# The first load of a row-maximum kernel in two halves of 64 partitions, issued from two queues

## The chip, the cores and the metric

The kernel runs on one core of one Trainium2 chip. The metric is the device time of one execution in microseconds (us). Three runs of the kernel before took 627.81 to 627.84 us, with a median of 627.82 us. The profile is of one further execution, which took 627.6 us.

## The reference

The input `x` is an 8192 x 8192 matrix of float32, 268.4 MB. The output has one number for each row: the largest absolute value in the row.

```python
def reference(x: np.ndarray) -> np.ndarray:
    return np.linalg.norm(x, ord=np.inf, axis=1)
```

So every byte of `x` has to be read once from device memory (HBM), and little is written: 32 KB.

## The kernel before

**Tiling.** On-chip memory (SBUF) has 128 partitions. The 8192 rows are taken in two groups (`GROUPS`): the first gives each partition 46 rows that follow each other in memory, the second 18. So each partition has 64 rows of 8192 numbers to work through, and what it reads for one load is one contiguous piece of memory. A "load" is a DMA of `w` numbers for every partition. The table `WHOLE` has 31 loads of 16384 numbers (two rows for each partition, 64 KB for each partition, 8.39 MB in all) and one of 8192. The table `LAST` cuts the last row of each partition into six shrinking loads of 3920 down to 320 and 352 numbers.

**Ring.** The data go to `ring`, a buffer of three slots of 64 KB for each partition, so three loads can be on their way or in use at once. The last piece of all goes to a small buffer, `last`. `load` (L97 on) finds the place in the ring, issues the DMA from SP's queue (L108), and keeps a list `loads` of the place and instruction of each load.

**Work.** For each whole load, VectorE (DVE) takes the largest absolute value of each row with one reduce (`absmax`, L68) over 128 x 16384 numbers. It writes two columns of `res`, which holds one result for each of the 64 rows of a partition. For the last two whole loads and for the pieces of the last row, `shared` splits the columns: DVE takes some, and ScalarE (ACT) makes the others absolute (L90) for GpSimd (POOL), which takes their maximum (L75). At the end one reduce joins the parts of the last row (`absmax` over `last`), SP writes its result column (L154) and ScalarE's queue writes the other 63 columns (L159).

**Order.** The engines' orders are those of the program (`keep`). SP does nothing but issue loads and the last store, in order. The first three loads wait for nothing. Each later load waits until the reduce that used its ring slot, three loads before, is over. A scheduler assigns the semaphores: DMAs take eight semaphores in turn, and an instruction that needs the data of a load waits for that load's semaphore. For some loads, chosen by `(len(loads) + 4) % 10 < 5`, the kernel declares that the new load need not wait for the earlier loads of the same slot themselves (the reduces in between order them); for the others SP has such a wait too, in an instruction of its own ahead of the load. ScalarE's first work is the load of its function table and one tiny activation (L140), which is made to wait for the second reduce, so that the table is there long before it is used at the end.

Of the kernel before, what the change touches and what calls it, by code (L numbers as in the profile page):

```python
# [1 line left out]

# [4 lines left out]

P = 128
FP32 = mybir.dt.float32
INT32 = mybir.dt.int32  # L10
MAX = mybir.AluOpType.max
X = mybir.AxisListType.X
ABS = mybir.ActivationFunctionType.Abs

GROUPS = [46, 18]


WHOLE = (
    [(16384, ())] * 30 + [(16384, (3712, 3680)), (8192, (2016, 1984))]
)
LAST = [
    (3920, (1680,)), (1984, (848,)), (1040, (432,)), (576, (240,)), (320, ()), (352, ())
]
RING = 3 * 16384


@with_exitstack  # L30
def kernel(
    ctx: ExitStack,
    tc: tile.TileContext,
    x: bass.AP,
    out: bass.AP,
):
    nc = tc.nc
    n_rows, n_cols = x.shape
    R = n_rows // P
    assert R == sum(GROUPS) and n_cols == 8192  # L40
    keep = tc.keep_in_program_order


    first = []
    x_of, out_of = {}, {}
    for k in GROUPS:
        f = len(first)
        x_of[f] = x[f * P : (f + k) * P].rearrange("(p r) m -> p (r m)", r=k)
        out_of[f] = out[f * P : (f + k) * P].rearrange("(p r) -> p r", r=k)
        first += [f] * k  # L50

    single = ctx.enter_context(tc.tile_pool(name="single", bufs=1))

    ring = single.tile([P, RING], FP32)
    res = single.tile([P, R], FP32)

    n_parts = sum(1 + len(g) for w, g in LAST[:-1])
    last = single.tile([P, LAST[-1][0] + n_parts], FP32)

    def not_before(inst, other, why):  # L60
        tc.add_manual_dep(
            inst.ins, other.ins.name,
            mybir.DependencyInfo(mybir.DependencyClass.Sync, mybir.DependencyReason.DATA),
            reason=why,
        )

    def absmax(dst, src):
        return keep(nc.vector.tensor_reduce(  # L68
            out=dst, in_=src, axis=X, op=MAX, apply_absolute_value=True,
        ))  # L70

    def max_pool(dst, src):

        pool = nc.gpsimd
        keep(pool.add_instruction(  # L75
            mybir.InstTensorReduce(
                name=nc.get_next_instruction_name(),
                ins=[pool.lower_ap(src.bitcast(INT32))],
                outs=[pool.lower_ap(dst.bitcast(INT32))],
                op=MAX,  # L80
                axis=X,
            )
        ))

    def shared(part, buf, g):

        a = buf.shape[1] - sum(g)
        red = absmax(part[:, :1], buf[:, :a])
        for i, c in enumerate(g):
            keep(nc.scalar.activation(buf[:, a : a + c], buf[:, a : a + c], ABS))  # L90
            max_pool(part[:, 1 + i : 2 + i], buf[:, a : a + c])
            a += c
        return red

    loads = []

    def load(pos, w):  # L97

        row = pos // n_cols
        a = pos - first[row] * n_cols  # L100
        if pos + w == R * n_cols:
            buf = last[:, :w]
        else:
            at = loads[-1][0] + loads[-1][1] if loads else 0
            if at + w > RING:
                at = 0
            buf = ring[:, at : at + w]
        inst = nc.sync.dma_start(out=buf, in_=x_of[first[row]][:, a : a + w]).ins  # L108
        if pos + w < R * n_cols:
            if (len(loads) + 4) % 10 < 5:  # L110


                for b, v, earlier in loads:
                    if b < at + w and at < b + v:
                        tc.declare_no_dep(
                            inst, earlier, reason="ordered by the reduces in between",
                        )
            loads.append((at, w, inst))
        return buf


    pos = 0
    for u, (w, g) in enumerate(WHOLE):
        buf = load(pos, w)
        row, k = pos // n_cols, w // n_cols
        pos += w
        whole = k - 1 if g else k
        if whole:
            red = absmax(
                res[:, row : row + whole],  # L130
                buf[:, : whole * n_cols].rearrange("p (c m) -> p c m", m=n_cols),
            )
        if g:
            part = single.tile([P, 1 + len(g)], FP32, name=f"part{u}")
            shared(part, buf[:, whole * n_cols :], g)
            max_pool(res[:, row + whole : row + k], part)
        if u == 1:

            not_before(
                keep(nc.scalar.activation(res[:, :1], res[:, :1], ABS)),  # L140
                red, "not before the second row is in",
            )


    n = LAST[-1][0]
    for h, (w, g) in enumerate(LAST[:-1]):
        buf = load(pos, w)
        pos += w
        shared(last[:, n : n + 1 + len(g)], buf, g)
        n += 1 + len(g)  # L150

    load(pos, LAST[-1][0])
    absmax(res[:, R - 1 :], last)
    final = nc.sync.dma_start(out=out_of[first[-1]][:, GROUPS[-1] - 1 :], in_=res[:, R - 1 :])  # L154


    for f, o in out_of.items():
        k = min(o.shape[1], R - 1 - f)
        early = keep(nc.scalar.dma_start(out=o[:, :k], in_=res[:, f : f + k]))  # L159
    tc.add_manual_dep(  # L160
        early.ins, final.ins.name,
        mybir.DependencyInfo(mybir.DependencyClass.NoSync, mybir.DependencyReason.SCHED_ONLY),
        reason="takes the later semaphore",
    )


# [1 line left out]
_INS = ['x']  # L168
_OUTS = [((8192,), 'float32')]


# [23 lines left out]
```

## Time and profile before

| what | value |
|---|---|
| median of three runs | 627.82 us |
| profiled execution, whole time | 627.6 us |
| profiled execution, span | 625.8 us |
| VectorE busy | 536.5 us, 86% of the span |
| ScalarE busy, GpSimd busy | 15.0 us, 14.1 us |
| moved by DMA | 268.47 MB, mean 429 GB/s |
| share of the 16 DMA engines' span that SP's queue took | 99.3% |
| one reduce of 128 x 16384 numbers | 17.22 us |
| issue of a load to its landing, median | 40.8 us |

The span is the time between the first and the last record of the core; the 1.8 us between it and the execution's time lie around it. "Busy" is the time in which an engine worked on an instruction; for DMA it is the time that packets took on the 16 DMA engines which all queues of the core share. A reader should keep in mind that a load's time to landing includes the time for which it stands behind earlier loads.

### The profile page before, as it was taken

What the parts mean: (1) busy time and instruction counts of PE and PEld (TensorE: products, weight loads), DVE (VectorE), ACT (ScalarE), POOL (GpSimd) and SP (SyncE); (2) the same over time, 40 slices, a digit from 0 to 9 for tenths busy, and PEclk for the clock granted to TensorE, in tenths of its full rate; (3) what the DMA queues carried; (4) which work ended last, traced back from release to release, by engine and by line L of the source; (5) the groups of instructions that cost most, each with busy time, mean ns of one, the idle gap of its engine ahead of it and who ended that gap; (6) DMA issues with size and microseconds to landing.
All of it is one profiled execution on the core that took longest, in us unless ns stands there. A gap on an engine that the chain in (4) does not pass through costs nothing.

```text
span 625.8 us, 173 instructions
## 1 busy us (share of the span) xinstructions
DVE 536.5 (86%) x39; ACT 15.0 (2%) x10; POOL 14.1 (2%) x14
## 2 busy tenths in 40 slices
DVE  0588988889888899888898888988889888899888
ACT  0000000000000000000000000000000000000044
POOL 0000000000000000000000000000000000000026
DMA  9999999999999999999999999999999999999997
GB/s 402 402 469 402 469 402 469 402 469 402 465 406 457 415 431 440 411 461 402 469 402 469 402 469 402 465 406 461 411 448 423 419 452 406 465 402 469 402 436 304
DMA packets 5904, 268.47 MB, mean 429 GB/s; under 512 B 1040, under 2 KB 1296, under 8 KB 1680
## 3 DMA queue, kind: packets, MB, share of 16 engines
q1 hardware_dynamic: 5616, 268.44, 99.3%
q10 hardware_dynamic: 288, 0.03, 0.0%
HBM read 268.44 MB, written 0.03 MB: 429 GB/s over the span
## 4 chain that ended last, share of the span: by engine, by line
DMA 71%; DVE 28%; SPq 0%; issue 0%; DVEq 0%
DMA ring<-in_x_dram 71%; DVE res L68 28%; DVE last L68 1%; SPq L108 0%; DVEq L68 0%
## 5 line engine op out<-in xcount | busy, mean ns | idle before, releaser
L68 DVE TENSOR_REDUCE res<-ring 128x2 f32<-128x16384 f32 (+1 forms) x31 | 525.3, 16944 | 86.7 <-DMA ring<-in_x_dram 86.7
L90 ACT ACTIVATE ring<-ring 128x3712 f32<-128x3712 f32 (+7 forms) x8 | 13.6, 1718 | 549.3 <-DMA ring<-in_x_dram 549.2
L75 POOL TENSOR_REDUCE part<-ring 128x1 int32<-128x3712 int32 (+3 forms) x4 | 10.1, 2562 | 607.8 <-ACT ring L90 607.8
L68 DVE TENSOR_REDUCE part<-ring 128x1 f32<-128x800 f32 (+1 forms) x2 | 5.5, 2748 | 0.1
L68 DVE TENSOR_REDUCE last<-ring 128x1 f32<-128x2240 f32 (+4 forms) x5 | 5.3, 1115 | 0.1
L75 POOL TENSOR_REDUCE last<-ring 128x1 int32<-128x1680 int32 (+3 forms) x4 | 3.4, 855 | 0.5 <-ACT ring L90 0.4
L140 ACT ACTIVATE res<-res 128x1 f32<-128x1 f32 x1 | 0.2, 202 | 57.3 <-DVE res L68 57.3
L140 ACT ACT_TABLE_LOAD x1 | 1.3, 1283 | 0.7 <-PEq L179 0.7
L68 DVE TENSOR_REDUCE res<-last 128x1 f32<-128x361 f32 x1 | 0.5, 529 | 0.1
L75 POOL TENSOR_REDUCE res<-part 128x1 int32<-128x3 int32 x2 | 0.4, 198 | 0.1
L179 POOL MEMSET const-float32-0.0<- 128x1 f32 x1 | 0.1, 100 | 0.2 <-issue 0.2
L179 POOL MEMSET const-bfloat16-1.0<- 128x1 bf16 x1 | 0.1, 103 | 0.0
L179 POOL MEMSET const-uint8-127<- 128x1 uint8 x1 | 0.1, 102 | 0.0
L179 POOL MEMSET const-float32-1.0<- 128x1 f32 x1 | 0.1, 99 | 0.0
## 6 DMA issues: line engine op xcount, KB each, us to landing
ring<-in_x_dram SPq DMA_DIRECT2D x1, 4096.0 KB, 31.2
ring<-in_x_dram SPq DMA_DIRECT2D x1, 1960.0 KB, 35.4
ring<-in_x_dram SPq DMA_DIRECT2D x1, 992.0 KB, 37.4
ring<-in_x_dram SPq DMA_DIRECT2D x1, 520.0 KB, 38.2
ring<-in_x_dram SPq DMA_DIRECT2D x31, 40.8
ring<-in_x_dram SPq DMA_DIRECT2D x1, 288.0 KB, 38.4
last<-in_x_dram SPq DMA_DIRECT2D x1, 176.0 KB, 38.3
ring<-in_x_dram SPq DMA_DIRECT2D x1, 160.0 KB, 38.3
```

Of the source, the lines that this page charges most:

```text
L68: return keep(nc.vector.tensor_reduce(out=dst, in_=src, axis=X, op=MAX, apply_absolute_value=True,))
L75: keep(pool.add_instruction(mybir.InstTensorReduce(name=nc.get_next_instruction_name(), ins=[pool.lower_ap(src.bitcast(INT32))], outs=[poo ...
L90: keep(nc.scalar.activation(buf[:, a : a + c], buf[:, a : a + c], ABS))
L140: keep(nc.scalar.activation(res[:, :1], res[:, :1], ABS)),
L179: nc = _bacc.Bacc("TRN2", target_bir_lowering=False, num_devices=1)
```

## The change

The first load alone is issued in two DMAs. The half for partitions 64 to 127 is issued by ScalarE's queue, ahead of ScalarE's table load, and the half for partitions 0 to 63 by SP, as SP's first DMA. Neither waits for anything. All other loads are as before, on SP's queue with 128 partitions. The list `loads` gets an entry for each half, so its length is greater by one for every later load, and so is the count of DMAs that take semaphores in turn: the choice `(len(loads) + 4) % 10 < 5` falls one load earlier, and each load's semaphore is the next one. The first reduce waits for two semaphores where it waited for one.

```diff
-        inst = nc.sync.dma_start(out=buf, in_=x_of[first[row]][:, a : a + w]).ins
+        src = x_of[first[row]][:, a : a + w]
+        n = P
+        if not loads:
+
+            n = P // 2
+            inst = nc.scalar.dma_start(out=buf[n:], in_=src[n:]).ins
+            loads.append((at, w, inst))
+        inst = nc.sync.dma_start(out=buf[:n], in_=src[:n]).ins
         if pos + w < R * n_cols:
             if (len(loads) + 4) % 10 < 5:
```

## The prediction

> **What bounds the kernel now.** I read the page's shares first, then the chain that ended last, then the waits, then the start. The page's parts 1 to 3:
>
> ```profile
> span 625.8 us, 173 instructions
> DVE 536.5 (86%) x39; ACT 15.0 (2%) x10; POOL 14.1 (2%) x14
> DMA  9999999999999999999999999999999999999997
> q1 hardware_dynamic: 5616, 268.44, 99.3%
> ```
>
> Transfers fill every slice; no compute engine does. The chain in order of time seems to say otherwise:
>
> ```profile
> 1.17 40.91 DMA ring<-in_x_dram
> 42.07 0.02 issue
> 42.10 17.23 DVE res L68
> 59.33 0.02 issue
> 59.34 40.77 DMA ring<-in_x_dram
> 100.11 0.02 issue
> 100.14 17.23 DVE res L68
> ...
> 582.18 35.44 DMA ring<-in_x_dram
> 617.63 0.02 issue
> 617.65 5.29 DVE last L68 x5
> ```
>
> It alternates, but one turn is 100.14 - 42.10 = 58.04 us for three loads, 19.35 us each: 8.39 MB / 19.35 us = 433.6 GB/s. A reduce takes 17.22 us. The chain passes through a reduce only because it releases the ring slot; the load issued then still stands behind 2.13 us of one load and all 19.35 us of the next, so 40.8 us to landing = 2.1 + 19.35 + 19.35. DVE is the one that waits:
>
> ```profile
> DVE res L68 <- DMA ring<-in_x_dram: 86.7, 31, 22.7
> SPq L108 <- DVE res L68: 526.2, 29, 19.0
> ```
>
> 86.7 us = 22.75 us for the first load and 30 waits of 2.13 us. So the bound is the DMA engines' own work: a microsecond more of it is a microsecond more in the end, and SP's waits for reduces are covered by about 21.5 us of queued work. The start:
>
> ```profile
> 0.73 1.28 ACT L140 ACT_TABLE_LOAD   x1 [0.73 <-PEq L179]
> 0.74 1.33 SPq L108 DMA_DIRECT2D ring<-in_x_dram  x3
> 22.75 17.22 DVE L68 TENSOR_REDUCE res<-ring 128x2 f32<-128x16384 f32 x1 [22.75 <-DMA ring<-in_x_dram]
> ```
>
> SP issues its three free loads within 1.33 us, and ScalarE comes to its first instruction at the same time, 0.73 us. In the trace's packet records each engine moves one partition's 64 KB at a time, eight per load, one after another: 19.35 / 8 = 2.42 us each. The first packets start at 1.83 to 2.34 us over the 16 engines, and an engine's second some 3.06 us after its first: a fill of about 0.64 us, paid once.
>
> [...]
> [...]
> [...]
> [...]
> [...]
>
> **The change part by part.**
>
> *Issue.* One SP issue of 64 rows for one of 128; one more on ScalarE. SP's take 0.33 to 0.43 us, ScalarE's two at the end 0.86 together, so 0.43. It stands ahead of the table load, which moves from 0.73 to about 1.16 us; behind that is only the activation at 59.35, which waits 57.34 us for a DVE reduce. Cost 0; uncovered it would be 0.43. The halves start side by side, so at most the later half's issue, under 0.5 us, could be lost or won at the start, out of 1.8 us before the first packet. I take 0.
>
> *The transfer of the first load.* The same 8.39 MB, eight packets per engine, now four from each queue. [...]a packet takes 2 x 2.42 = 4.84 us, eight take 38.7 us in place of 19.35. That is +19.3 us. [...]I take the middle, +18.2. The unknown is bounded below by 0 (full rate; a gain is excluded, since the rest of the kernel already shows the full rate) and above by 19.3 and another fill, about 20.
>
> [...]A load has landed when its slowest engine is done, and every later load again gives that engine its sixteenth, with no gap in which to catch up.
>
> *Where the delay goes.* The first reduce starts at about 41 us and ends at 58 in place of 40. Load 3, which waits for it, is late by 18.2 too. But loads 1 and 2, issued by 2.1 us, stand in SP's queue and are late by the same, so load 3 still finds 21.5 us ahead of it. No second loss, no recovery: the 2.13 us that DVE has to spare per load help nothing, since DMA is the bound.
>
> *Two semaphores for the first reduce.* One more wait instruction on DVE, whose like on SP takes 17 ns where it finds its semaphore ready: 0.02 us once, within the 2.13 us of DVE's waiting.
>
> *Shifted waits and semaphores.* In the built program SP's loads have the same kinds of waits, the undeclared ones one load earlier; each is for a DMA of eight, or three, loads before, whose data a past reduce has already used. The last store waits for the same load as before. ScalarE's first L90 and GpSimd's first L75 gain waits for the two halves, past for 560 us. SP's 14 extra wait instructions stand before loads which have 21.5 us of cover. Cost 0; uncovered, up to 14 x 1.74 us, the longest of them.
>
> *The tail* (from 617.65 on) has the same instructions, later by 18.2.
>
> Sum on the profiled execution: 627.6 + 0 + 18.2 + 0 = 645.8 us. The median of the runs lies 0.2 above it, so 646.0.
>
> **The rivals.**
>
> *A, the likeliest[...]*, 646.0, own range 643 to 648[...]. [...]Against: nothing in this trace shows sharing.
>
> *B, not slower[...].* [...]Then the load takes 19.35 us and the time is 627.8, give or take 0.5.[...]
>
> *C, a part: changing queues costs[...].* If there is no conflict, but an engine pays the fill of 0.64 us anew at each of seven changes: +4.5 us, 632.3.[...] Against the first: packets of one queue follow each other without a gap. Range 630.5 to 643.
>
> *D: ScalarE's half starts late* and takes turns with load 1 instead. Load 0 then lands later, but the bytes are the same; up to some 20 us of it changes only DVE's start, as SP's queue holds loads 1 and 2. [...]627.8; I put it with B.
>
> *E, faster:* only what lies before the first packet could go, 1.8 us, and splitting leaves most of it. By over 0.2% (1.25 us) hardly possible.
>
> **How the numbers follow.** A 0.68, C 0.12, B and D 0.18, E 0.02. A measurement of this kernel can tell about 0.2%, 1.25 us. A and C are slower by more than that: 0.80; same 0.18; faster 0.02. The time is A's, 646.0. A and C together are 0.80, so the range is theirs with a little above A's end, 630.5 to 648.5; B is left out.
>
> **What would show it.** Right: the first reduce starts near 41 us (between 38 and 43), the page's first two slices show about 230 GB/s instead of 402, a queue of ScalarE's has 4.19 MB more, packets of the first load take up to 4.8 us; then the waits of 2.13 us, the turn of 58.04 us and the five last reduces as before, only later. The DMA digits should stay 9[...]. B: the first reduce at 22.7 us, all else unmoved. C: between. Wrong in another way: a wait of 2.13 us that changed in the middle of the kernel, or a gap in the slices, which would mean that the shifted waits count; or a first reduce that is late while the end is not (D).

## The result, and the profile after

The changed kernel takes 647.76 us (median of five runs, 647.59 to 648.71) against 627.82 for the kernel before: a ratio of 1.0323, with a 95% interval from 1.0308 to 1.0337. It is slower by 19.9 us. The profiled execution took 647.65 us, with a span of 645.9 us, 20.1 us more than before.

The page's parts 1 to 3, with the moved GB/s of each fortieth of the span:

```profile
span 645.9 us, 177 instructions
DVE 536.5 (83%) x39; ACT 15.1 (2%) x10; POOL 14.2 (2%) x14
DMA  9979999999989999999999999999999999999997
GB/s 195 260 260 455 446 398 455 451 394 455 455 390 455 455 390 455 455 394 451 455 394 451 455 406 438 455 414 430 455 426 418 455 434 410 455 434 410 455 412 304
q1 hardware_dynamic: 5552, 264.24, 96.2%
q10 hardware_dynamic: 368, 4.23, 3.0%
```

The rate of the kernel before:

```profile
GB/s 402 402 469 402 469 402 469 402 469 402 465 406 457 415 431 440 411 461 402 469 402 469 402 469 402 465 406 461 411 448 423 419 452 406 465 402 469 402 436 304
```

The compute engines work as long as before (DVE 536.5 us in both). The DMA engines look as busy as before, too, and yet they move 195 and 260 GB/s in the first two slices, where it was 402 in each. The 7 in the third slice is no pause: the page counts a packet in the slice in which it starts, and in the packet records all 16 engines are busy throughout that slice. A busy digit tells that packets are under way, not how fast they move: in the stretches below, a share of 0.97 goes with 219 GB/s and with 415. ScalarE's queue, q10, now has 4.19 MB of the input.

The same two stretches of the kernel before and of the changed one show where all of it lies. The columns are the stretch, its length, the busy time of DVE, ACT and POOL with the number of instructions, the clock, the DMA share and the GB/s. First the kernel before:

```profile
0.00:43.00 43.00, 18.12 (x2) 1.28 (x1) 0.20 (x4) 1.00 0.97 415
43.00:600.00 557.00, 497.33 (x29) 0.20 (x1) 0.00 (x0) 1.00 1.00 434
```

And the changed kernel:

```profile
0.00:43.00 43.00, 0.17 (x1) 1.28 (x1) 0.20 (x4) 1.00 0.97 219
43.00:600.00 557.00, 497.53 (x29) 0.20 (x1) 0.00 (x0) 1.00 1.00 433
```

The first 43 us move 219 GB/s instead of 415 at the same DMA share; everything after runs at the old rate (433 and 434 GB/s). The timeline of the changed kernel at its start and the chain at its end:

```profile
0.73 1.65 SPq L115 DMA_DIRECT2D ring<-in_x_dram  x3
0.74 0.56 ACTq L113 DMA_DIRECT2D ring<-in_x_dram  x1
1.33 1.28 ACT L147 ACT_TABLE_LOAD   x1 [1.33 <-PEq L186]
42.83 17.22 DVE L68 TENSOR_REDUCE res<-ring 128x2 f32<-128x16384 f32 x1 [42.83 <-DMA ring<-in_x_dram]
61.97 17.22 DVE L68 TENSOR_REDUCE res<-ring 128x2 f32<-128x16384 f32 x1 [1.92 <-DMA ring<-in_x_dram]
```

```profile
602.08 35.45 DMA ring<-in_x_dram
637.53 0.02 issue
637.55 5.30 DVE last L68 x5
```

The first reduce starts at 42.83 us, 20.08 later than before. The second waits 1.92 us (before: 2.13), so 0.2 of that came back. The last pieces' reduces start 19.90 us later and take the same 5.3 us. The trace also has a record of every packet, which the page does not show. In these packet records, the packets of load 0 after each engine's first took:

```
                 packets took, min / median / max    first 16 packets start    load 0's last packet ends
kernel before            2.42 / 2.42 / 2.42 us           1.74 to 2.25                 22.4
changed kernel           4.84 / 4.85 / 5.00 us           2.07 to 3.06                 41.9
```

In the changed kernel each of the 16 engines takes a packet of SP's queue first, then one of ScalarE's, and so on, four of each. So all engines work on the same half, except for the 1.3 us over which their changes from one queue to the other are spread. Each packet takes twice the time of before (4.85 us for 2.42). Only the first packets do not: before, the first took 3.16 us on average, 0.7 more than the others, and now it takes 4.88, hardly more than the others. The extra time comes up in the first packets of load 1 instead, which take 3.05 us for 2.42.

### The profile page after: what moved, and what is told of

Same layout as the page of the kernel before. It is cut to its first block, busy times and chain, and to the rows that moved or that the text cites. A ratio compares the mean times of both kernels' runs of the same rounds, so it can differ in the third digit from the quotient of the medians.

```text
span 645.9 us, 177 instructions
## 1 busy us (share of the span) xinstructions
DVE 536.5 (83%) x39; ACT 15.1 (2%) x10; POOL 14.2 (2%) x14
## 4 chain that ended last, share of the span: by engine, by line
DMA 69%; DVE 30%; another core or an unknown queue 0%; issue 0%; SPq 0%; DVEq 0%
DMA ring<-in_x_dram 69%; DVE res L68 29%; DVE last L68 1%; SPq L115 0%; DVEq L68 0%
## 5 line engine op out<-in xcount | busy, mean ns | idle before, releaser
L75 POOL TENSOR_REDUCE part<-ring 128x1 int32<-128x3712 int32 (+3 forms) x4 | 10.1, 2561 | 627.7 <-ACT ring L90 627.7
L147 ACT ACTIVATE res<-res 128x1 f32<-128x1 f32 x1 | 0.2, 203 | 76.6 <-DVE res L68 76.6
```

Source lines behind the costliest of these rows:

```text
L75: keep(pool.add_instruction(mybir.InstTensorReduce(name=nc.get_next_instruction_name(), ins=[pool.lower_ap(src.bitcast(INT32))], outs=[poo ...
```

## The experiments

Theory T is that of the prediction: with 64 neighbouring partitions a packet takes 4.84 us, twice the 2.42 of the kernel before; carried on to 16 neighbours, four times. The factors were my estimate; no trace of the kernel before shows them. It has two forms. In one, the form of reach, the time follows from which partitions a DMA writes in all, neighbours or spread ones; in the other, fixed pairs of engines slow each other while they are in step, and these pairs, too, were my assumption. Its rivals are that two queues cost something by taking turns (Q), that ScalarE's queue is slow (R), that the late landing itself costs (L), or that the rows read lie badly in HBM (S). Other letters are explained in the expectation where they come up, and hold for it alone. The code shows the lines that matter: a line with a minus is one of the changed kernel's, and where there is none, the lines with a plus take the place of the first load's DMA or, where the text says so, stand ahead of it. Where no interval is given, the time is that of one run; the kernel before stayed between 627.33 and 627.98 us in all its runs, so 20 us are far outside the noise.

**One queue for both halves.**

```diff
-            inst = nc.scalar.dma_start(out=buf[n:], in_=src[n:]).ins
+            inst = nc.sync.dma_start(out=buf[h:], in_=src[h:]).ins   # after SP's buf[:h]
```

> The first load in the same two halves of 64 partitions, both issued by SP, 0 to 63 first. Theory T ([...]a packet takes 4.84 us in place of 2.42): the halves follow each other instead of taking turns, each at half rate, 8 x 4.84 = 38.7 us for the load, so about 627.8 + 19.3 = 647.1 us, first reduce at about 42. Theory Q (taking turns between two queues costs 2.4 us a packet): one queue, no turns, 627.8 us. Theory R (ScalarE's queue is slow or late): 627.8 us.

Measured: 649.19 us.

```profile
44.66 17.22 DVE L68 TENSOR_REDUCE res<-ring 128x2 f32<-128x16384 f32 x1 [44.66 <-DMA ring<-in_x_dram]
```

The slow load stays without ScalarE's queue and without turns, so Q and R fall as causes of it. It is even slower than the changed kernel by 1.4 us: most packets took 5.12 us here, 4.85 there. So the two halves under way at once do a little better than one after the other.

**Halves by columns.** Both DMAs have 128 partitions and half the columns.

```diff
+            h = w // 2
+            inst = nc.scalar.dma_start(out=buf[:, h:], in_=src[:, h:]).ins
+            inst = nc.sync.dma_start(out=buf[:, :h], in_=src[:, :h]).ins
```

> The first load in two halves by columns (128 partitions x 8192 numbers each), one issued by ScalarE, one by SP. Theory T: [...]two queues cost nothing: 627.8 us within 0.5, first reduce at about 23. Theory Q: 16 packets of 32 KB an engine take turns, each at half rate: 647 us. Theory R: more than 627.8, up to 647.

Measured: 627.55 us against 627.56 for the kernel before beside it, ratio 1.0000 (0.9991 to 1.0008). The first reduce, from the timeline:

```profile
22.99 17.22 DVE L68 TENSOR_REDUCE res<-ring 128x2 f32<-128x16384 f32 x1 [22.99 <-DMA ring<-in_x_dram]
```

Two queues, ScalarE's among them, taking turns on the same 16 engines, cost nothing here that can be measured, and gain nothing. Packets of 32 KB took 1.21 us.

**The whole first load on ScalarE's queue.**

```diff
+            inst = nc.scalar.dma_start(out=buf, in_=src).ins   # the first load, all 128 partitions
```

> The first load whole (128 partitions) on ScalarE's queue, the rest on SP's. It takes turns with load 1, so load 0 should land at about 40 us as the halves did, with load 1 at about the same time. Theory T: [...]the bytes per engine are the same, the late first landing is not what costs: 627.8 us within 0.5. Rival L (what costs is that the first reduce starts 20 us late): 647. Theory Q: 16 turns at half rate, 660 or more.

Measured: 628.94 us, ratio 1.0027 (1.0015 to 1.0038). The first reduce is nearly as late as in the changed kernel, but the end moves by 1.4 us, not 20. From the chain and the waits:

```profile
0.73 41.24 DMA ring<-in_x_dram
41.97 0.02 issue
41.99 137.11 DVE res L68 x8
```

```profile
DVE res L68 <- DMA ring<-in_x_dram: 88.7, 23, 42.0
```

```profile
41.99 154.23 DVE L68 TENSOR_REDUCE res<-ring 128x2 f32<-128x16384 f32 x9 [41.99 <-DMA ring<-in_x_dram]
198.22 17.22 DVE L68 TENSOR_REDUCE res<-ring 128x2 f32<-128x16384 f32 x1 [2.00 <-DMA ring<-in_x_dram]
```

So L falls: a first landing at 42 us cost 1.4 us here, where the engines moved 419 GB/s or more in every 20 us from 40 to 200. DVE runs nine reduces without a pause, and regains some 2.2 us with each of the eight after the first, since a load takes that much longer than a reduce (19.35 us and 17.1). The 1.4 us is a miss of the expectation. Load 3 could only be issued at 59.24 us, when the engines had 1.1 to 1.5 us of queued packets left, and its first packets began 1.4 to 2.4 us after that. In the packet records an engine stood idle for 0.42 us on average around 60 us, the worst for 1.29, and the first packet after it took 3.1 us on average instead of 2.42. The cushion of 21.5 us was just used up.

**Even and odd partitions in place of low and high.**

```diff
-            inst = nc.scalar.dma_start(out=buf[n:], in_=src[n:]).ins
+            inst = nc.scalar.dma_start(out=buf[1::2], in_=src[1::2]).ins
-        inst = nc.sync.dma_start(out=buf[:n], in_=src[:n]).ins
+            inst = nc.sync.dma_start(out=buf[0::2], in_=src[0::2]).ins
```

> The first load in two halves of 64 partitions, even partitions by SP, odd ones by ScalarE's queue. [...]Theory T in its form of pairs in step: [...]4.84 us a packet, 647.5 us. Theory T in its form of reach[...]: 627.8.

Measured: 627.76 us (the kernel before beside it 627.56, 627.33 to 627.74).

```profile
23.12 17.22 DVE L68 TENSOR_REDUCE res<-ring 128x2 f32<-128x16384 f32 x1 [23.12 <-DMA ring<-in_x_dram]
```

This is the changed kernel with the same two queues, the same bytes and 64 partitions to each DMA; only which partitions differs. The loss is gone. So it isn't the width of 64 nor the number of DMAs. What is left is where the partitions lie, or which source rows are read together, which the next run tells apart. Theory T's form of reach (627.8 us) held, and its form of pairs in step (647.5), with the split among engines that I had assumed, did not.

**The source in even and odd rows, the destination in halves.** The first two results of each partition are then those of other rows.

```diff
-            inst = nc.scalar.dma_start(out=buf[n:], in_=src[n:]).ins
+            inst = nc.scalar.dma_start(out=buf[h:], in_=src[1::2]).ins
-        inst = nc.sync.dma_start(out=buf[:n], in_=src[:n]).ins
+            inst = nc.sync.dma_start(out=buf[:h], in_=src[0::2]).ins
```

> The two halves of the change (64 partitions each, SP and ScalarE), but partitions 0 to 63 get the even rows of the source and 64 to 127 the odd ones, so the first two results of each partition are those of other rows. [...]Theory T[...]: the destination is the same, so 647.7 us. Theory S (rows that are read at one time lie badly in HBM): 627.8, or another time well off 647.7.

Measured: 647.70 us.

```profile
43.24 17.22 DVE L68 TENSOR_REDUCE res<-ring 128x2 f32<-128x16384 f32 x1 [43.24 <-DMA ring<-in_x_dram]
```

Its DMAs read the same rows as those of the run on even and odd partitions, and write elsewhere. One is 20 us slower than the other (647.70 and 627.76 us), so here it is the destination that decides, and S falls.

**Eight DMAs of 16 partitions.**

```diff
+            for p in range(0, P, 16):
+                inst = nc.sync.dma_start(out=buf[p : p + 16], in_=src[p : p + 16]).ins
```

> The first load in eight DMAs of 16 partitions each, all issued by SP, in order: one row for each engine. Theory T[...]: [...]a packet takes 4 x 2.42 = 9.67 us, eight take 77.4 in place of 19.35: 627.8 + 58 = 686 us, first reduce at about 80. Theory H (an engine is slower by a fixed factor of two when a transfer is narrower than 128 partitions, whoever else writes): 647 us. Theory of fixed cost per DMA: seven more DMAs of under 1 us, 628 to 635.

Measured: 682.36 us, 54.8 more than before; first reduce at 77.35; packets of 9.26 us, 3.8 times those of before, where theory T had four times and 686 us. The page's rate by slices:

```profile
GB/s 123 123 123 123 247 432 432 432 432 432 432 432 432 439 432 435 443 435 439 451 435 435 432 432 432 432 432 432 432 432 432 432 432 432 432 432 432 432 432 310
```

With 16 neighbours at a time the load moves at a little over a quarter of the rate (123 GB/s, where 432 is the whole), and all of the delay reaches the end: the first reduce is 54.6 us later than in the kernel before, the end 54.8.

**Four pieces, without and with a lag between the engines.** If the fixed pairs of theory T slowed each other only while both were in the same half, keeping eight engines one piece behind should bring the full rate back. Two spare packets for each of the eight, 2 x 2.42 = 4.84 us, were to do that: the time of one piece at the full rate.

```diff
+            for r in (0, 1):                      # only with the lag
+                o = slice(r, r + 32, 4)
+                nc.sync.dma_start(out=ring[o, 2 * w :], in_=x_of[0][o, 2 * w : 3 * w])
+            for c in range(0, w, w // 2):
+                for p in (h, 0):
+                    o = (slice(p, p + h), slice(c, c + w // 2))
+                    inst = nc.sync.dma_start(out=buf[o], in_=src[o]).ins
```

> The first load in four DMAs, all issued by SP: partitions 64 to 127 then 0 to 63 of the first 8192 columns, then the same of the second. Each engine has four packets of 32 KB in each. Theory T: [...]each piece takes 9.7 us, four take 38.7: 647 us. Theory H the same.

> As the kernel with four pieces, and ahead of them two more DMAs of 8 rows of 64 KB each (spare copies of part of load 2, on partitions 0, 4 ... 28 and 1, 5 ... 29)[...]. [...]Theory T: [...]the load takes 19.35 us after the added 4.84, so 627.8 + 4.8 = 632.7 us, some 14.5 less than without the added work. Theory H (each engine is slow by itself in a transfer of 64 partitions) and theory S: 647 + 4.8 = 652 us.

Measured: 648.56 us without the lag, 1.6 over the expectation, and 656.45 with it, where theory T had 632.7. The records have the lag: the engines with spare packets come to their first packet of the load at 9.1 to 10.1 us, the others at about 5.0. Yet the packets of 32 KB took 2.4 to 2.6 us, twice their 1.21, from then on to the end of the load; only the first of each of the eight engines without the lag took less, 1.8 to 2.1. So the lag gained nothing. Whether it stood between the two engines of each pair that I had assumed, the records cannot tell, as they have no engine numbers. The spare packets themselves show something the theory does not explain: the first of each engine took 2.7 to 3.2 us, the second, begun together with the other engines' first pieces, 4.0 to 4.5, though it went to partitions below 64 while these pieces went to those from 64 on.

**Which partitions slow each other.** Spare DMAs ahead of the kernel before, one at a time.

```diff
+            for k, d in tests:                    # k partitions, d apart, from partition 0 on
+                o = slice(0, (k - 1) * d + 1, d)
+                keep(nc.sync.dma_start(out=ring[o, 2 * w :], in_=x_of[0][o, 2 * w : 3 * w]))
```

> The kernel before with 27 spare DMAs ahead of it, one at a time (each waits for the one before to land), each of k partitions d apart from partition 0 on, 64 KB to a partition; they copy parts of load 2, which is loaded again afterwards. [...]Theory N[...]: k = 2 slow at d = 1 to 4 only, k = 8 slow by two at d = 4 and fast at 8, k = 16 fast at d = 8; 64 partitions slow with d = 1 and fast with d = 2. Theory E (no sharing by partition, the split among engines decides): no k = 2 slow. The sum of the tests is some 150 to 220 us on top of 627.8.

Measured: 851.74 us in all; the tests took 224 us. The longest packet of each test, from the packet records:

```
k = 2    d:   1    2    3    4    8    16   20   24   28   32   36   64   96
        us:  5.0  5.3  4.9  3.4  3.3  3.4  3.4  3.6  3.6  4.1  3.4  3.6  2.8
k = 8    d:   1    2    4    8    16        k = 16   d:   1    2    4    8
        us:  9.1  5.0  3.3  5.2  5.6                us:  9.4  5.2  5.4  5.5
k = 32   d = 1: 11.0 us in all, mean packet 4.96     d = 4:  6.0 us, mean packet 2.79
k = 64   d = 1: 21.2 us in all, mean packet 5.09     d = 2: 10.9 us, mean packet 2.57
k = 128  d = 1: 20.4 us in all, mean packet 2.49
```

With two partitions, a packet took 4.9 to 5.3 us where the other partition was 1, 2 or 3 from partition 0, and 2.8 to 3.6 at all the other distances tried but 32. There the test is not clear: 4.1 us lies between the two. But 8 partitions at a spacing of 8 or 16, and 16 at 4 or 8, took 5.2 to 5.6 us, though two partitions alone took 3.3 to 3.4 at each of these spacings. All these sets hold partitions 32 apart; 8 partitions at a spacing of 4, the only set of 8 that was fast (3.3 us), do not. The 32 partitions at a spacing of 4 hold some, too, and had a mean packet of 2.79 us; the records don't tell which of their packets ran together. Theory N, a guess that any eight neighbours slow each other, had 8 partitions slow at a spacing of 4 and 16 fast at 8; they took 3.3 and 5.5 us, so it falls. So does E, which had no slow pair. The test of 64 partitions with d = 2 (mean packet 2.57 us) confirms the run on even and odd partitions. It contradicts the split that I had assumed, four successive rows of the 64 to an engine: then the first packets of 64 even partitions would go to partitions 0, 8, 16 and so on, and 16 packets to just those took 5.5 us.

**The halves in the middle.** Load 15 in place of the first.

```diff
-        if not loads:
+        if len(loads) == 15:
```

> The same two halves of 64 partitions, SP and ScalarE, but of load 15, in the middle of the kernel; the first load is whole again. Theory P ([...]its bytes move at half rate, and nothing later can catch up): 8 x 2.43 = 19.4 us more than before, so 627.5 + 19.4 = 646.9 us, wherever the load stands; ScalarE's half takes turns with load 14 and so is not moved together with SP's half, but each still pays 9.7. Rival B (the loss needs both halves at once, as at the start): between 627.5 and 637. Rival W (in the middle other waits give it back): less than 640.

Measured: 650.33 us, 22.9 more than before (627.39). The reduce of load 14 and the next, from the timelines of the kernel before (the first two lines) and of this one:

```profile
293.65 17.22 DVE L68 TENSOR_REDUCE res<-ring 128x2 f32<-128x16384 f32 x1 [2.13 <-DMA ring<-in_x_dram]
313.01 17.22 DVE L68 TENSOR_REDUCE res<-ring 128x2 f32<-128x16384 f32 x1 [2.13 <-DMA ring<-in_x_dram]
315.48 17.22 DVE L68 TENSOR_REDUCE res<-ring 128x2 f32<-128x16384 f32 x1 [24.10 <-DMA ring<-in_x_dram]
335.83 17.22 DVE L68 TENSOR_REDUCE res<-ring 128x2 f32<-128x16384 f32 x1 [3.13 <-DMA ring<-in_x_dram]
```

The waits of 2.13 us have become 24.10 and 3.13, 22.97 us more, and no more than 0.1 of it is regained: B and W fall. ScalarE's half, in turns with load 14, had packets of 4.6 to 5.3 us, and SP's, alone, of 4.4 to 5.2. By the packet records ScalarE's four packets cost an engine 10.3 us more than at 2.42 each, SP's four 10.4, the four of load 14 that took turns with ScalarE's 1.6 (2.6 to 3.1 us each), and load 16's first 0.6: 22.9 in all. So the 3.4 us above the expectation lie in packets of about 5.0 us in place of 4.85, and in packets of other loads where an engine goes from a half to a whole load.

## Why the prediction was right, and where it was not

- **What bounds the kernel.** Right. DMA alone sets the time, and nothing catches up: time lost by the DMA engines stands in the end, from the start (19.9 us) as from the middle (22.9).
- **The rate of the halves.** Right in its size, but the factor of two for a packet of a half was an estimate that no trace of the kernel before shows. The runs measured it: 4.85 us a packet for 2.42 with 64 neighbouring partitions, 9.26 with 16, and with two partitions 4.9 to 5.3 us at distances of 1 to 3, 4.1 at 32 and 2.8 to 3.6 at the others tried. Two DMAs on even and odd partitions had the full rate (627.76 us). Why neighbours are slower, no run shows.
- **The size.** 18.2 us was predicted, 19.9 came. The mis-sized term is the transfer of the first load. I had started from 4.84 us for a packet of one half, +19.3 us for the load, and taken off 1.1 us for a gain from two halves at once, an estimate that no trace had shown. The packets took 4.85 us, so the eight cost 8 x (4.85 - 2.42) = 19.4 us. That looks like no help at all, but the start was too low: a half by itself took 5.12 us a packet with one queue and 5.09 on average in the test of 64 neighbours. Against 5.12, the 4.85 of two halves at once is a gain of 5.6%. My reason for a gain, a lag between the engines, isn't borne out: from the second packet on the engines' starts lay 1.28 us apart from first to last, and yet none of these packets was shorter than 4.84 us. What makes one half by itself slower than 4.84, and two at once a little faster, is open. The start, put at 0, cost 0.4 us on average: a DMA of 64 rows took 0.55 to 0.56 us to issue, not 0.33 to 0.43, and the first packets began at 2.07 to 3.06 us instead of 1.74 to 2.25 (the prediction's 1.83 to 2.34 for the kernel before was counted from a zero 0.09 us off). The two make 19.8 of the 19.9 us.
- **Which engines slow each other.** Not shown, and as far as tested wrong. I had assumed fixed pairs of engines, so that a lag between the two would help. The run on even and odd partitions (627.76 us, where pairs in step had 647.5) and the tests of 64 partitions contradict it, and so does the run with the lag (656.45 us for 632.7) if the lag was where I had meant it. How a DMA of 64 rows is split over the engines is still open, and so is why the spare packets were slowed. The time came out right all the same, as in every turn all 16 engines worked on the same half of 64 neighbours, and such a packet took 4.85 us. Each of them took SP's packet first. I had assumed this order, but nothing in the trace of the kernel before showed it, so in this part the prediction was lucky.
- **Where the delay goes.** Right: loads 1 and 2 are as late as load 0, so load 3 had its cushion, and the waits of 2.13 us returned after one of 1.92.
- **Edits at no cost.** Right. The table load moved to 1.33 us under a wait of 76.6, and SP's waits for earlier loads, 43.4 us before and 63.0 after, grew by the late first load alone.
- **Rivals.** B, which had the first load at 19.35 us, did not happen: no engine took ScalarE's packet first, and the load's packets ran from 2.07 to 41.9 us. Of C, the run by columns shows that changing queues costs nothing by itself (627.55 us for 627.56). D's late landing at the full rate is the run with the whole load on ScalarE's queue: hidden but for 1.4 us, where I had called it free up to some 20 us; the time from the issue to the first packets, 1.4 to 2.4 us there, has to be left in the cushion.

## What to carry to other kernels

In a kernel bound by transfers, expect no gain from splitting a load over queues where the engines are busy already (here 627.55 us for 627.56), and look at the partitions of each part for what a split may cost. Cut by columns, or into every second partition, the parts kept the full rate here (627.55 and 627.76 us); cut into blocks of 64 or 16 neighbours, a packet took 4.85 or 9.26 us in place of 2.42 (647.76 and 682.36 us). A DMA share of 0.97 stood beside 219 GB/s and beside 415, so the GB/s of the same stretch belongs beside the share. And ask of a delay whether it takes time from the bottleneck or only moves a landing: 20 us of the first cost 20, and 19 us of the second 1.4.

## What the runs showed of the hardware

- 64 neighbouring partitions took 4.85 us for a packet of 64 KB when two queues took turns (one half each), and 5.12 us when one queue moved one half after the other. I had expected the same for both.
- 64 partitions two apart were as fast per packet as 128 neighbours (mean 2.57 and 2.49 us with the first fill, in the test of single DMAs), and 32 partitions four apart nearly so (2.79), where 32 neighbours took 4.96.
- The longer first packet of a full-rate load (3.16 us for 2.42, on average) has no like in a half of 64 neighbours (4.88 for 4.85); it is paid where the engines go back to a whole load (3.05 in load 1).
- The time to issue a DMA does not follow from its rows alone: the halves took 0.55 to 0.56 us, and so did the whole load that SP issued right after its half (0.56); the whole loads of the kernel before took 0.38 to 0.43 at the start and 0.33 later; single DMAs of 8 rows took 0.30 to 0.68.
